# A hybrid encoder in one kernel: the swapped B table's copies moved behind x's evictions, and another order of y, layer norm, gelu and the first output projection

## The chip, the cores and the metric

The kernel runs on one core of a Trainium2 chip, as one program. The metric is the device time of one execution in microseconds (us); less is better. The kernel before takes 1248.14 us (median of 3 runs, 1248.09 to 1248.31). A difference of 0.2%, about 2.5 us, is what a measurement of this kernel can tell from no change.

Names: PE is TensorE, DVE is VectorE, ACT is ScalarE, POOL is GpSimd, and SP is the engine whose queue starts most transfers. Each engine works through its own instructions in the order of the program; a wait of one instruction holds all that stand behind it on the same engine.

## What is computed

Two layers over 512 tokens of 1024 channels, each followed by a gated feed-forward block of width 2816. Only the first layer's mixer matters here. Cut to that:

```python
def conv_ssm_layer(h, w_in, ...):
    z = h @ w_in                                   # 512 x 1536
    za, zg, u = z[..., :512], z[..., 512:1024], z[..., 1024:]
    ya = conformer_conv(za, zg, ...)               # silu(layer_norm(conv31(za * sigmoid(zg)) + conv_b))
    yb = s5_mixer(u, ...)                          # two scans (forward, backward), gelu, gated linear unit
    return jnp.concatenate([ya, yb], axis=-1) @ w_out

def s5_mixer(u, ...):
    y = y_fwd + y_bwd + d_skip * u
    y = gelu(y)
    return y * sigmoid(y @ glu_w + glu_b)
...
x = x + conv_ssm_layer(rms_norm(x, g), ...)
x = x + swiglu_ffn(rms_norm(x, f), ...)            # then layer 1: neighbourhood attention, and swiglu again
```

Here `h = rms_norm(x, mix_norm[0])`; the kernel scales by the norm after the projection.

## The kernel before

The order on each engine is written out by hand in the code: the framework keeps the order of issue. Matmuls of the later part are done as three products of two halves, high and low (`mm3`, L200 to L203: high by high, low by high, high by low), so each weight chunk is split into `whi` (ACT, L91) and `wlo` (DVE, L93) by `Weights.split`; the twelve chunks of the input projection are used whole, straight from the transfer (`wraw`, three buffers, loaded by SP, L74).

**The start.** `x` comes in as four slices (two tiles named `U` and `an`); the transfers of `x` are issued first, then three weight chunks, then the small tables (`b`, vectors, `c`). `g_params` on DVE works out the state-space coefficients, a chain of about a hundred small operations; its last six (`g_cmul`, L437) make the table `bb`. Two ACT copies then make `bbs`, the table with real and imaginary part exchanged and one sign turned (L568, L569). Behind the call of `g_params` in the program stand 32 transposes of `x` on PE into eight PSUM tiles (L617), and for each of these tiles two ACT evictions: `xg` (scaled by the norm's gain, L620) and `xT` (kept for the residual, L621). The first projection `u` (L668) takes `xg`, four weight chunks and four PSUM tiles that the first four of the eight give up. After the first chunk's turn come four squares on ACT (L662) for the norm's `rsqrt` on DVE, after the second `make_pb(0)` to `make_pb(2)` on DVE (three operations each, L437), which read `bb` and `bbs`, and `piece_t` on PE (L630), which reads `pb`.

**The middle.** Scans, the other two projections (`zg`, `za`, L731) and the tables of the convolution run interleaved, until `an` goes through 64 transposes into `AC` and the convolution runs on PE (L994), four blocks of four groups.

**Behind the convolution.** During the convolution DVE works on `Q`, eight pieces of three operations each (`fused`, L437), the tables of the SSM's output. How many go between two of its other instructions is set by a credit in nanoseconds, `tick(TCONV)` per group, and by `bgV.finish(piece)` where a piece is needed. Each block of the convolution is evicted by DVE with a sum for the layer norm (L1004, L1006). Then:

- `out_y(i, hq)`, four times: 24 matmuls of T and Q against U and the states (L1023, L1026) and one ACT eviction into `yn` (L1029).
- `ln_mean`: four small matmuls `mean` (L1065), two DVE subtractions (L1069), eight ACT squares (L1073). `ln_scale`: one small matmul `var` (L1078), `rsqrt` of twelve DVE operations, then eight scalings, five on DVE (L1084) and three on ACT (L1082).
- `out_t(ct)`: eight transposes `yT` (L1091) and an ACT eviction into `yg`, which has `AC`'s buffer (L1038).
- `out_a(ct)`: eight transposes `cT` (L1091), ACT's Silu (L1101), the high half `mah` (DVE for three of four, L1104, ACT for the last, L1106) and the low half `mal` (DVE, L1107).
- `gelu(c1, c2)`: six steps for two channel tiles in lockstep, alternating between ACT and DVE (L1044 to L1054); it ends with `ygh` (ACT) and `ygl` (DVE), which the trace both calls `ygs`.
- `out_half(p, mah, mal, ...)`: 24 matmuls `wo` of one weight chunk. Then 48 matmuls `glu`, in two chunks of 24, which read `ygs`.

The order of the last ones is written in `MIDS = (2, 0, 3, 1)`: gelu of tiles 0 and 2, half 0, gelu of tiles 1 and 3, half 1; the glu's matmuls take the tiles in the order 0, 2, 1, 3.

```python
    for ct in (0, 2, 1, 3):
        out_t(ct)
    for ct in range(4):
        out_a(ct)
    ...
    for v in MIDS:
        if v < 2:
            out_half(v, mah, mal, True, psa)
        else:
            gelu(*((0, 2), (1, 3))[v - 2])
```

Of the kernel before, what the change touches and what calls it, by code (L numbers as in the profile page):

```python
# [9 lines left out]
F32 = mybir.dt.float32  # L10
F32R = mybir.dt.float32r
I32 = mybir.dt.int32
AF = mybir.ActivationFunctionType
ALU = mybir.AluOpType
# [5 lines left out]

CAP = 3000.0
HV = (4, 4)
TCONV = 1900
TCV = 10
QN, QT = 0, 2
LN, LT, LV = 1, 4, 6
LNA, MAH = (1, 3, 5), (0, 1, 2)
KW, VW = 64, 64
ZT, ZC = 500, -1000
MIDS = (2, 0, 3, 1)  # L30

P = 128
D = 1024
KD = 8
S = 512
# [81 lines left out]
def tile_hybrid_encoder(ctx, tc, x, mix_norm, ffn_norm, ffn_w_gate, ffn_w_up, ffn_w_down,  # L117
# [5 lines left out]
    V, A, PE, PL = nc.vector, nc.scalar, nc.tensor, nc.gpsimd  # L123
# [73 lines left out]
    def tmp(shape, tag, bufs=2, dt=F32):  # L197
        return sm.tile(shape, dt, tag=tag, name=tag, bufs=bufs)
# [120 lines left out]
    bgV = Background(1.0)  # L319
# [10 lines left out]
    mp = mixp.enter_context(tc.tile_pool(name="mp", bufs=1))  # L330
# [174 lines left out]
    def g_params():  # L505
        lr, li = par[:, 0], par[:, 1]
        dt = pg()
        th, si, co = (pg(3 * G).rearrange("p (a g) -> p a g", a=3) for _ in range(3))
        x1 = pg(2 * G).rearrange("p (a g) -> p a g", a=2)
        yield from g_exp(dt, par[:, 2], G)  # L510
        yield tt(x1[:, 0], lr, dt, ALU.mult)
        yield tt(th[:, 0], li, dt, ALU.mult)
        yield ts(x1[:, 1], x1[:, 0], float(LCH), None, ALU.mult, None)
        for i in (1, 2):
            yield ts(th[:, i], th[:, 0], float(LCH ** i), None, ALU.mult, None)
        yield from g_lockstep(g_exp(*(v.rearrange("p a g -> p (a g)") for v in (m8, x1)), 2 * G),
                              g_sincos(*(v.rearrange("p a g -> p (a g)") for v in (si, co, th)), 3 * G))
        V.memset(pw[:, 0, 0], 1.0)
        V.memset(pw[:, 1, 0], 0.0)
        ar, ai = pw[:, 0, 1], pw[:, 1, 1]  # L520
        yield tt(ar, m8[:, 0], co[:, 0], ALU.mult)
        yield tt(ai, m8[:, 0], si[:, 0], ALU.mult)
        V.memset(et[:, 0, 0], 1.0)
        V.memset(et[:, 1, 0], 0.0)
        V.tensor_copy(out=et[:, 0, 1], in_=co[:, 1:3])
        V.tensor_copy(out=et[:, 1, 1], in_=si[:, 1:3])
        t1, t2, den, cr, ci, pr = (pg() for _ in range(6))
        t3, t4 = pg(), pg()
        u1, u2 = (pg(4 * G).rearrange("p (e g) -> p e g", e=4) for _ in range(2))

        def g_coef():
            yield tt(den, lr, lr, ALU.mult)
            yield tt(t1, li, li, ALU.mult)
            yield ts(pr, ar, 1.0, None, ALU.subtract, None)
            yield tt(den, den, t1, ALU.add)
            yield tt(t1, pr, lr, ALU.mult)
            yield tt(t2, ai, li, ALU.mult)
            V.reciprocal(out=den, in_=den)
            yield 280
            yield tt(t3, ai, lr, ALU.mult)  # L540
            yield tt(t4, pr, li, ALU.mult)
            yield tt(t1, t1, t2, ALU.add)
            yield tt(t3, t3, t4, ALU.subtract)
            yield tt(cr, t1, den, ALU.mult)
            yield tt(ci, t3, den, ALU.mult)

        def g_pow():
            for base, n in ((1, 1), (2, 2), (4, 4)):
                sh = [P, n, G]
                br, bi = (pw[:, q, base].unsqueeze(1).to_broadcast(sh) for q in range(2))  # L550
                yield from g_cmul(pw[:, 0, base + 1:base + 1 + n], pw[:, 1, base + 1:base + 1 + n],
                                  pw[:, 0, 1:1 + n], pw[:, 1, 1:1 + n], br, bi, u1[:, 0:n], u2[:, 0:n])

        yield from g_lockstep(g_coef(), g_pow())
        f, b = slice(0, 64), slice(64, 128)
        for q in range(2):
            V.tensor_copy(out=pwP[f, q].rearrange("p g (t j) -> p j t g", t=2),
                          in_=pw[f, q, 7::-1].rearrange("p (j t) g -> p j t g", t=2))
            yield cost(256)
            V.tensor_copy(out=pwP[b, q].rearrange("p g (t j) -> p j t g", t=2),  # L560
                          in_=pw[b, q, 0:8].rearrange("p (j t) g -> p j t g", t=2))
            yield cost(256)
        yield from g_phase()
        sh = [P, G, 16]
        w1, w2 = pbt(sh), pbt(sh)
        yield from g_cmul(bb[:, :, 0], bb[:, :, 1], cr.unsqueeze(2).to_broadcast(sh),
                          ci.unsqueeze(2).to_broadcast(sh), braw[0], braw[1], w1, w2)
        A.activation(out=bbs[:, :, 0], in_=bb[:, :, 1], func=AF.Copy, scale=-1.0)  # L568
        A.activation(out=bbs[:, :, 1], in_=bb[:, :, 0], func=AF.Copy)  # L569

    def g_phase():

# [83 lines left out]
    for i in range(4):  # L656
        w = W.next()
        W.ahead()
        if i == 0:
            ss = tmp([P, 4], "hrs", 1)  # L660
            for j in range(4):
                A.activation(out=un.rearrange("p g j c -> p (g j c)")[:, 0:D], in_=xn[j], func=AF.Square,  # L662
                             accum_out=ss[:, j:j + 1])
        for kk in range(2):
            k = 2 * i + kk
            for j in range(4):
                c = slice(j * P, (j + 1) * P)
                PE.matmul(out=pu[j], lhsT=xg[:, k, c], rhs=w[:, kk], start=(k == 0), stop=(k == 7))  # L668
# [25 lines left out]
        if i == 2:  # L694
            for r in range(2):
                ps = psb("ct")
                for t in range(4):
# [3 lines left out]
                             scale=-1.0 if r else 1.0)  # L701
# [103 lines left out]
    S2 = pt([P, 2, G, NCH], "S2")  # L805
# [206 lines left out]
    def out_y(i, hq, between=None):  # L1012
        for key in ((i, hq), (i + 2, hq)):
            if key in job_q:
                bgV.finish(job_q[key])
        ps = psb("y")
        for gi in range(4):
            if gi == 2 and between is not None:
                between()
            gs = [h * 16 + i * 8 + hq * 4 + gi for h in range(2)]  # L1020
            o = [ps[64 * h:64 * h + 64, gi * P:(gi + 1) * P] for h in range(2)]
            for h, g in enumerate(gs):
                PE.matmul(out=o[h], lhsT=U[:, g], rhs=T[:, :, g], start=True, stop=False)  # L1023
            for r in range(2):
                for h, g in enumerate(gs):
                    PE.matmul(out=o[h], lhsT=S2[:, r, g],  # L1026
                              rhs=Q[g // 8][:, hq, r, gi].rearrange("p t c -> p (t c)"),
                              start=False, stop=(r == 1))
        A.activation(out=yn[:, :, i * 8 + hq * 4:i * 8 + hq * 4 + 4],  # L1029
                     in_=ps.rearrange("p (g t c) -> p t g c", g=4, t=LCH), func=AF.Copy)  # L1030
# [4 lines left out]
    def out_t(ct):  # L1035
        ps = psb("yT")
        chan(yn, ct, ps)
        A.activation(out=yg[:, ct], in_=ps, func=AF.Copy)  # L1038
# [17 lines left out]
    def gelu(*cts):  # L1056
        for _ in g_lockstep(*(g_gelu(ct) for ct in cts)):
            pass
# [35 lines left out]
    def mix_tile(n):  # L1094
        return lp.tile([P, 4, S], F32R, tag="Q", name=n, bufs=4)

    def out_a(ct):
        ps = psa("cT")
        chan(yc, ct, ps)
        y = tmp([P, S], ("sq", "sqacc")[ct % 2])  # L1100
        A.activation(out=y, in_=ps, func=AF.Silu, scale=col[:, R_LG + ct:R_LG + ct + 1],  # L1101
                     bias=col[:, R_LB + ct:R_LB + ct + 1])
        if ct in MAH:
            V.tensor_copy(out=mah[:, ct], in_=y)  # L1104
        else:
            A.activation(out=mah[:, ct], in_=y, func=AF.Copy)  # L1106
        V.tensor_tensor(out=mal[:, ct], in0=y, in1=mah[:, ct].bitcast(F32), op=ALU.subtract)  # L1107

    out_y(0, 0)
    bgV.finish(job_q[1, 0])  # L1110
    ln_mean()
    out_y(0, 1)
    out_y(1, 0)
    out_y(1, 1)
    ln_scale()
    ygs = mp.tile([P, 2, 4, S], F32R, tag="S2", name="ygs")
    ygh, ygl = ygs[:, 0], ygs[:, 1]
    mah, mal = mix_tile("mah"), mix_tile("mal")
    for ct in (0, 2, 1, 3):
        out_t(ct)  # L1120
    for ct in range(4):
        out_a(ct)

    po = {}

    def out_half(p, mh, ml, first, ps_of=None):
        wh, wl = W.next()
        W.ahead()
        for mi in range(2):
            m = 2 * p + mi  # L1130
            if first:
                po[m] = ps_of("wo")
            c = slice(mi * P, mi * P + P)
            for k in range(4):
                mm3(po[m], wh[:, k, c], wl[:, k, c], mh[:, k], ml[:, k], first and k == 0,
                    not first and k == 3)

    for v in MIDS:
        if v < 2:
            out_half(v, mah, mal, True, psa)  # L1140
        else:
            gelu(*((0, 2), (1, 3))[v - 2])
    mbh, mbl = mix_tile("mbh"), mix_tile("mbl")
    for p2 in range(2):
        wh, wl = W.next()
# [403 lines left out]
```

## Time and profile before

| | |
|---|---|
| median of 3 runs | 1248.14 us (1248.09 to 1248.31) |
| the profiled execution, its own time | 1248.74 us |
| its span, first to last instruction | 1247.0 us |
| PE busy | 1198.9 us, 96% of the span |
| DVE busy | 664.7 us, 53% |
| ACT busy | 474.9 us, 38% |
| POOL busy | 40.2 us, 3% |
| DMA, mean rate | 95 GB/s |

How to read it: of the span, 48 us are left in which PE has no matmul, and the page's forty slices of 31 us show where: PE's digit is 2 in the first slice and 7 in the sixth and seventh, about 156 to 218 us; elsewhere it is 9, but for an 8 in the last. Both places that the change touches lie in these slices. A busy PE is not one at its peak: the granted clock stands beside it, in tenths 7 in the first slice, 8 in the sixth and 7 in the seventh, 9 elsewhere.

### The profile page before, as it was taken

To read this page: it belongs to the slowest core of one execution; us is meant where nothing else is said; L and a number is where in the kernel's file an instruction comes from. 1 tells how busy PE (TensorE), PEld (TensorE's weight loads), DVE (VectorE), ACT (ScalarE), POOL (GpSimd) and SP (SyncE) were. 2 spreads that over 40 slices of the span, in tenths; PEclk is the share of its full clock that TensorE was granted. 3 is DMA by queue.
4 is the path that set the end of the run, shared out by engine and by line. 5 is a ranking of instruction groups with operands and counts; after the bars stand their busy time and mean duration, and the time that the engine had idled before them with its cause. 6 is when DMAs were issued, how large, how long until landed. Compare 5 with 4: busy or idle time off the path is not lost.

```text
span 1247.0 us, 16100 instructions
## 1 busy us (share of the span) xinstructions
PE 1198.9 (96%) x6427; PEld 952.8 (76%) x6427; DVE 664.7 (53%) x1113; ACT 474.9 (38%) x837; POOL 40.2 (3%) x90
## 2 busy tenths in 40 slices
PE   2999977999999999999999999999999999999998
PEld 2465566888888888888888887678888888888886
DVE  8489986675444444433336753766544444442322
ACT  0667484543323223222225455744322332221120
POOL 1100100000000000000000001520000000000000
PEclk7999987999999999999999999999999999999999
DMA  7411231333333333233344453313333333323321
GB/s 156 75 41 56 76 73 35 101 89 98 91 96 102 101 102 95 82 93 93 93 142 158 119 169 91 102 39 101 85 102 102 95 91 99 89 100 101 119 101 34
DMA packets 173154, 118.04 MB, mean 95 GB/s; under 512 B 21193, under 2 KB 153593, under 8 KB 173080
## 3 DMA queue, kind: packets, MB, share of 16 engines
q1 hardware_dynamic: 172616, 115.92, 32.1%
q10 hardware_dynamic: 400, 1.07, 0.4%
q8 instruction: 50, 0.82, 0.3%
q14 instruction: 24, 0.20, 0.1%
q0 software_dynamic: 64, 0.03, 0.0%
HBM read 109.04 MB, written 7.96 MB: 94 GB/s over the span
## 4 chain that ended last, share of the span: by engine, by line
PE 87%; DVE 10%; ACT 2%; issue 1%; DMA 0%; DVEq 0%; POOL 0%; POOLq 0%
PE up L201 6%; PE gate L203 6%; PE up L203 6%; PE gate L201 6%; PE gate L202 6%; PE up L202 6%; PE qkv L1414 4%; PE qkv L1416 4%; PE qkv L1415 4%; PE dn L203 3%; PE dn L201 3%; PE dn L202 3%; PE dn L1515 3%; PE dn L1513 3%; PE dn L1514 3%; DVE work L437 3%
## 5 line engine op out<-in xcount | busy, mean ns | idle before, releaser
L93 DVE TENSOR_TENSOR wlo<-wraw,whi 128x1024 fp32r<-128x1024 f32 x176 | 213.0, 1213 | 256.2 <-ACT whi L91 254.7
L91 ACT ACTIVATE whi<-wraw 128x1024 fp32r<-128x1024 f32 x176 | 183.5, 1044 | 282.3 <-issue 113.6
L201 PE MATMUL gate<-xgh,whi 128*128 128x512 f32 x352 | 137.2, 390 | 0.0
L201 PE MATMUL up<-xgh,whi 128*128 128x512 f32 x352 | 137.1, 390 | 0.0
L203 PE MATMUL gate<-xgh,wlo 128*128 128x512 f32 x352 | 137.0, 389 | 0.0
L203 PE MATMUL up<-xgh,wlo 128*128 128x512 f32 x352 | 137.0, 389 | 0.0
L202 PE MATMUL gate<-xgl,whi 128*128 128x512 f32 x352 | 136.9, 389 | 0.0
L202 PE MATMUL up<-xgl,whi 128*128 128x512 f32 x352 | 136.9, 389 | 0.0
L1198 DVE TENSOR_TENSOR fu<-up,rstdB 128x512 f32<-128x512 f32 x44 | 30.4, 691 | 113.4 <-PE up L203 113.4
L1200 ACT ACTIVATE gh<-fu 128x512 fp32r<-128x512 f32 x44 | 27.8, 632 | 151.2 <-DVE fu L1199 151.2
L203 PEld LDWEIGHTS up<-xgh,wlo 128*128 128x128 f32 x352 | 66.1, 188 | 13.7
L201 PEld LDWEIGHTS gate<-xgh,whi 128*128 128x128 f32 x352 | 66.1, 188 | 13.7
L202 PEld LDWEIGHTS up<-xgl,whi 128*128 128x128 f32 x352 | 66.1, 188 | 13.8
L202 PEld LDWEIGHTS gate<-xgl,whi 128*128 128x128 f32 x352 | 66.1, 188 | 13.7
L203 PEld LDWEIGHTS gate<-xgh,wlo 128*128 128x128 f32 x352 | 66.0, 188 | 13.8
L201 PEld LDWEIGHTS up<-xgh,whi 128*128 128x128 f32 x352 | 66.0, 188 | 13.6
L201 PE MATMUL dn<-gh,whi 128*128 128x512 f32 x176 | 69.3, 394 | 0.0
L202 PE MATMUL dn<-gl,whi 128*128 128x512 f32 x176 | 69.3, 394 | 0.0
L203 PE MATMUL dn<-gh,wlo 128*128 128x512 f32 x176 | 69.3, 394 | 0.0
L1515 PE MATMUL dn<-whi,gl 128*128 128x512 f32 x176 | 69.2, 393 | 0.0
L1513 PE MATMUL dn<-whi,gh 128*128 128x512 f32 x176 | 69.0, 392 | 0.0
L1414 PE MATMUL qkv<-whi,xgh 128*128 128x512 f32 x176 | 68.8, 391 | 0.0
(299 smaller groups left out, 2017.9 us busy)
## 6 DMA issues: line engine op xcount, KB each, us to landing
wraw<-in_ffn_w_gate_dram SPq DMA_DIRECT2D x44, 512.0 KB
wraw<-in_ffn_w_up_dram SPq DMA_DIRECT2D x44, 512.0 KB
wraw<-in_ffn_w_down_dram SPq DMA_DIRECT2D x38, 512.0 KB
wraw<-in_na_w_qkv_dram SPq DMA_DIRECT2D x24, 512.0 KB
wraw<-in_ab_w_in_dram SPq DMA_DIRECT2D x12, 512.0 KB
bt<-bd SPq DMA_DIRECT2D x8, 640.0 KB
wraw<-in_ab_w_out_dram SPq DMA_DIRECT2D x8, 512.0 KB
wraw<-in_na_w_out_dram SPq DMA_DIRECT2D x8, 512.0 KB
```

Source lines behind the costliest of these rows:

```text
L91: self.nc.scalar.activation(out=hi, in_=raw, func=AF.Copy)
L93: eng.tensor_tensor(out=lo, in0=raw, in1=hi.bitcast(F32), op=ALU.subtract)
L201: PE.matmul(out=o, lhsT=lh, rhs=rh, start=start, stop=False)
L202: PE.matmul(out=o, lhsT=lh, rhs=rl, start=False, stop=False)
L203: PE.matmul(out=o, lhsT=ll, rhs=rh, start=False, stop=stop)
L437: V.tensor_tensor(out=o, in0=a, in1=b, op=op)
L1414: PE.matmul(out=pq[j], lhsT=lh, rhs=wh[:, kk], start=(k == 0), stop=False)
L1415: PE.matmul(out=pq[j], lhsT=lh, rhs=wl[:, kk], start=False, stop=False)
L1416: PE.matmul(out=pq[j], lhsT=ll, rhs=wh[:, kk], start=False, stop=(k == 7))
L1513: PE.matmul(out=pd[j], lhsT=gh[:, k, c], rhs=wh[:, kk], start=(k == 0), stop=False)
L1514: PE.matmul(out=pd[j], lhsT=gh[:, k, c], rhs=wl[:, kk], start=False, stop=False)
L1515: PE.matmul(out=pd[j], lhsT=gl[:, k, c], rhs=wh[:, kk], start=False, stop=(k == NF - 1))
```

## The change

1. The two copies of `bbs` are taken out of `g_params` and issued on ACT behind the evictions of `x` and the four squares.
2. `TCONV` goes from 1900 to 2200, so more pieces of `Q` stand between the convolution's groups.
3. Behind the convolution `out_y(1, 1)`, the `yT` transposes and both gelus are issued behind half 0; `ln_scale` and `out_a` move ahead of them. All four `mah` are made on ACT, and the four `mal` are issued on DVE together, behind the four.

```diff
-TCONV = 1900
+TCONV = 2200
...
-LNA, MAH = (1, 3, 5), (0, 1, 2)
+LNA = (1, 3, 5)
...
-MIDS = (2, 0, 3, 1)
...
         yield from g_cmul(bb[:, :, 0], bb[:, :, 1], cr.unsqueeze(2).to_broadcast(sh),
                           ci.unsqueeze(2).to_broadcast(sh), braw[0], braw[1], w1, w2)
-        A.activation(out=bbs[:, :, 0], in_=bb[:, :, 1], func=AF.Copy, scale=-1.0)
-        A.activation(out=bbs[:, :, 1], in_=bb[:, :, 0], func=AF.Copy)
...
             for j in range(4):
                 A.activation(out=un.rearrange("p g j c -> p (g j c)")[:, 0:D], in_=xn[j], func=AF.Square,
                              accum_out=ss[:, j:j + 1])
+            A.activation(out=bbs[:, :, 0], in_=bb[:, :, 1], func=AF.Copy, scale=-1.0)
+            A.activation(out=bbs[:, :, 1], in_=bb[:, :, 0], func=AF.Copy)
...
+    ya = {}
+
     def out_a(ct):
         ps = psa("cT")
         chan(yc, ct, ps)
-        y = tmp([P, S], ("sq", "sqacc")[ct % 2])
+        y = ya[ct] = tmp([P, S], ("sq", "sqacc")[ct % 2])
         A.activation(out=y, in_=ps, func=AF.Silu, scale=col[:, R_LG + ct:R_LG + ct + 1],
                      bias=col[:, R_LB + ct:R_LB + ct + 1])
-        if ct in MAH:
-            V.tensor_copy(out=mah[:, ct], in_=y)
-        else:
-            A.activation(out=mah[:, ct], in_=y, func=AF.Copy)
-        V.tensor_tensor(out=mal[:, ct], in0=y, in1=mah[:, ct].bitcast(F32), op=ALU.subtract)
+        A.activation(out=mah[:, ct], in_=y, func=AF.Copy)
+
+    def out_a_low(ct):
+        V.tensor_tensor(out=mal[:, ct], in0=ya.pop(ct), in1=mah[:, ct].bitcast(F32), op=ALU.subtract)
...
     out_y(1, 0)
-    out_y(1, 1)
     ln_scale()
-    ygs = mp.tile([P, 2, 4, S], F32R, tag="S2", name="ygs")
-    ygh, ygl = ygs[:, 0], ygs[:, 1]
     mah, mal = mix_tile("mah"), mix_tile("mal")
-    for ct in (0, 2, 1, 3):
-        out_t(ct)
     for ct in range(4):
         out_a(ct)
+    bgV.finish(job_q[1, 1])
+    for ct in range(4):
+        out_a_low(ct)
...
-    for v in MIDS:
-        if v < 2:
-            out_half(v, mah, mal, True, psa)
-        else:
-            gelu(*((0, 2), (1, 3))[v - 2])
+    out_half(0, mah, mal, True, psa)
+    out_y(1, 1)
+    ygs = mp.tile([P, 2, 4, S], F32R, tag="S2", name="ygs")
+    ygh, ygl = ygs[:, 0], ygs[:, 1]
+    for ct in (0, 2, 1, 3):
+        out_t(ct)
+    gelu(0, 2)
+    gelu(1, 3)
+    out_half(1, mah, mal, True, psa)
```

What this does to the order is shown at three places. The first is ACT at the start, before; the sixteen evictions alternate as their first two rows do.

```order
L608 ACTIVATE col<-vec_171 128x16
L568 ACTIVATE bbs<-bb 128x8x64
L569 ACTIVATE bbs<-bb 128x8x64
L620 ACTIVATE xg<-xT,col 128x512
L621 ACTIVATE xT<-xT 128x512
...
L662 ACTIVATE un_ppb,hrs<-U 128x1024 x2
L662 ACTIVATE un_ppb,hrs<-an 128x1024 x2
L682 ACTIVATE col<-vec 128x34
```

The same place with the change:

```order
L605 ACTIVATE col<-vec_171 128x16
L617 ACTIVATE xg<-xT,col 128x512
L618 ACTIVATE xT<-xT 128x512
...
L659 ACTIVATE un_ppb,hrs<-U 128x1024 x2
L659 ACTIVATE un_ppb,hrs<-an 128x1024 x2
L661 ACTIVATE bbs<-bb 128x8x64
L662 ACTIVATE bbs<-bb 128x8x64
L681 ACTIVATE col<-vec 128x34
```

The two copies have moved behind the evictions and the squares; nothing else moved on ACT there, and nothing on the other engines.

The second place is ACT behind the convolution, from the layer norm's scaling to the first gelu, before (`sq` and `sqacc` are the Silu's results, `AC` the evicted `yT`, `whi` the split of the next weight chunk).

```order
L1029 ACTIVATE yn<-y 128x8x64 x3
L1082 ACTIVATE an<-an,rs_y 128x256 x3
L1038 ACTIVATE AC<-yT 128x512 x4
L1101 ACTIVATE sq<-cT,col 128x512
L1101 ACTIVATE sqacc<-cT,col 128x512
...
L1106 ACTIVATE mah<-sqacc 128x512
L1044 ACTIVATE sq<-AC 128x512 x2
```

The same place with the change:

```order
L1028 ACTIVATE yn<-y 128x8x64 x2
L1081 ACTIVATE an<-an,rs_y 128x256 x3
L1102 ACTIVATE sq<-cT,col 128x512
L1104 ACTIVATE mah<-sq 128x512
L1102 ACTIVATE sqacc<-cT,col 128x512
L1104 ACTIVATE mah<-sqacc 128x512
...
L90 ACTIVATE whi<-wraw 128x1024
L1028 ACTIVATE yn<-y 128x8x64
L1037 ACTIVATE AC<-yT 128x512 x4
L1043 ACTIVATE sq<-AC 128x512 x2
```

The last `yn`, the four `AC` evictions and the gelu stand behind the four Silus now, each Silu has its `mah` behind it, and a weight split stands ahead of the last `yn`. On PE the order is correspondingly `var`, `cT`, 24 `wo`, the last 24 `y`, `yT`, 24 `wo`, `glu`, where it was the last `y`, `var`, `yT`, `cT`, 48 `wo`, `glu`.

The third place is DVE at the end of the convolution, from the weight splits on, before:

```order
L93 TENSOR_TENSOR wlo<-wraw,whi 128x1024 x2
L1004 TENSOR_TENSOR an<-conv,rstdB 128x8x64
L1006 TENSOR_REDUCE lns<-an 128x8
L437 TENSOR_TENSOR wq<-pwQ,CTs 128x1024
L437 TENSOR_TENSOR Q<-Q,wq 128x1024
L437 TENSOR_TENSOR Q<-pwQ,CT 128x1024
L1004 TENSOR_TENSOR an<-conv,rstdB 128x8x64
L1006 TENSOR_REDUCE lns<-an 128x8
L1069 TENSOR_TENSOR an<-an,mean 128x1024 x2
L437 TENSOR_TENSOR wq<-pwQ,CTs 128x1024
L437 TENSOR_TENSOR Q<-Q,wq 128x1024
```

The same place with the change:

```order
L92 TENSOR_TENSOR wlo<-wraw,whi 128x1024 x2
L1003 TENSOR_TENSOR an<-conv,rstdB 128x8x64
L1005 TENSOR_REDUCE lns<-an 128x8
L436 TENSOR_TENSOR wq<-pwQ,CTs 128x1024
L436 TENSOR_TENSOR Q<-Q,wq 128x1024
L1003 TENSOR_TENSOR an<-conv,rstdB 128x8x64
L1005 TENSOR_REDUCE lns<-an 128x8
L1068 TENSOR_TENSOR an<-an,mean 128x1024 x2
```

All 24 operations of `Q` now stand ahead of the mean's subtraction; two stood behind it. Of these, one operation now stands ahead of the first evicted block, a place where DVE waited, and one more of the 24 between the table of groups 10 and 11 (`tcb`) and the last evicted block.

## Rows read from the trace of the kernel before

**Rows 1.** The page's chain that ended last, by engine, whole span.
```profile
PE 87%; DVE 10%; ACT 2%; issue 1%; DMA 0%; DVEq 0%; POOL 0%; POOLq 0%
```

**Rows 2.** Windows: engine busy in each stretch, clock, DMA share, GB/s.
```profile
core 0: us, PE busy (x) PEld busy (x) DVE busy (x) ACT busy (x) POOL busy (x), PEclk, DMA share, GB/s
9.00:13.00 4.00, 3.89 (x19) 3.92 (x20) 3.93 (x27) 0.00 (x0) 0.00 (x0) 1.00 1.02 229
...
18.00:19.00 1.00, 0.00 (x0) 0.00 (x0) 0.93 (x5) 0.00 (x0) 0.00 (x0) 0.78 0.12 8
...
32.00:35.50 3.50, 3.50 (x4) 1.44 (x5) 0.00 (x0) 3.50 (x7) 0.00 (x0) 0.50 0.00 0
...
80.00:120.00 40.00, 40.00 (x351) 22.94 (x350) 38.96 (x45) 25.45 (x58) 0.00 (x0) 1.00 0.18 53
```

**Rows 3.** Timeline of ACT at the start: start us, duration us, instruction, [idle before].
```profile
29.72 0.63 ACT L568 ACTIVATE bbs<-bb 128x512 f32<-128x512 f32 x1 [22.57 <-DVE bb L437]
...
30.78 0.67 ACT L620 ACTIVATE xg<-xT,col 128x512 f32<-128x512 f32 x1
...
31.82 0.69 ACT L620 ACTIVATE xg<-xT,col 128x512 f32<-128x512 f32 x1
```

**Rows 4.** Timeline of PE at the start.
```profile
12.55 3.18 PE L617 MATMUL xT<-ident,an 128*128 128x128 f32 x16
31.99 15.79 PE L668 MATMUL u<-wraw,xg 128*128 128x512 f32 x32 [16.26 <-ACT xT L621]
...
56.10 1.04 PE L630 MATMUL P<-ident,pb 128*128 128x128 f32 x8
```

**Rows 5.** Timeline of DVE at the start.
```profile
43.99 0.17 DVE L220 TENSOR_SCALAR rs_a<-hrs 128x4 f32<-128x4 f32 x1 [14.30 <-ACT un_ppb L662]
...
46.45 1.22 DVE L437 TENSOR_TENSOR pb<-pwP,bb 128x1024 f32<-128x1024 f32 x1
```

**Rows 6.** Timeline of SP's queue at the start.
```profile
5.33 4.56 SPq L74 DMA_DIRECT2D wraw<-in_ab_w_in_dram  x3
```

**Rows 7.** Two tiles' instructions: duration ns min/median/max, first and last start us.
```profile
L617 PE MATMUL xT<-ident,U x16: 421/421/448, 9.1 to 12.3; 128*128 128x128 f32 x16
...
L630 PE MATMUL P<-ident,pb x24: 272/273/273, 56.1 to 76.0; 128*128 128x128 f32 x24
```

**Rows 8.** Timeline of PE behind the convolution.
```profile
193.20 0.59 PE L1065 MATMUL mean<-lns,wpad 128*128 128x8 f32 x2 [4.46 <-DVE lns L1006]
...
204.51 0.39 PE L1078 MATMUL var<-lnq,wpad 128*128 128x8 f32 x2
...
208.89 2.77 PE L1091 MATMUL cT<-ident,an 64*128 64x64 f32 x32 [2.43 <-DVE an L1084]
211.78 0.79 PE L201 MATMUL wo<-mah,whi 128*128 128x512 f32 x1
...
219.74 0.39 PE L201 MATMUL wo<-mah,whi 128*128 128x512 f32 x1
...
225.18 0.39 PE L201 MATMUL glu<-ygs,whi 128*128 128x512 f32 x1
```

**Rows 9.** Windows behind the convolution; columns as in rows 2.
```profile
190.00:199.00 9.00, 5.80 (x52) 5.78 (x54) 7.82 (x8) 3.30 (x16) 0.00 (x0) 0.50 0.09 31
...
209.00:216.50 7.50, 7.38 (x42) 5.86 (x43) 5.00 (x10) 6.74 (x13) 0.00 (x0) 0.55 0.00 0
```

**Rows 10.** Timeline of DVE behind the convolution.
```profile
196.10 1.22 DVE L437 TENSOR_TENSOR wq<-pwQ,CTs 128x1024 f32<-128x1024 f32 x1
...
223.35 1.29 DVE L1054 TENSOR_TENSOR ygs<-AC,ygs 128x512 fp32r<-128x512 f32 x2
```

**Rows 11.** Timeline of ACT behind the convolution.
```profile
208.57 2.03 ACT L1038 ACTIVATE AC<-yT 128x512 f32<-128x512 f32 x4
210.48 0.79 ACT L1101 ACTIVATE sq<-cT,col 128x512 f32<-128x512 f32 x1
...
213.90 1.35 ACT L1044 ACTIVATE sq<-AC 128x512 f32<-128x512 f32 x2
...
219.31 1.13 ACT L1044 ACTIVATE sq<-AC 128x512 f32<-128x512 f32 x2
```

## The prediction

> **What bounds the kernel now.** I read the page's chain first: PE carries 87% of it, DVE 10% [rows 1]. The page's slices show PE busy from the eighth on, so the later layers stay as they are. What can move lies in the stretches in which PE waits, and I read those in the timelines of the engines, with the windows beside them for the clock.
>
> Two places matter. At the start ACT sits idle for 22.57 us until DVE has made `bb`, because the two `bbs` copies stand at the head of its queue [rows 3]. The evictions of x stand behind them, although the transposes that fill their PSUM tiles ended at 15.73 us (12.55 + 3.18), and PE waits 16.26 us for the first pair [rows 4]. Behind the convolution PE waits for the layer norm: 4.46 us before the last `mean` matmuls and 2.43 us before `cT` [rows 8], and after such waits it works at half clock, 0.50 granted from 190 to 199 us and 0.55 from 209 to 216.5 us [rows 9], which is 1.2 GHz for nearly all of both.
>
> **Part 1, the copies of bbs.** They take 1.1 us of ACT and stay; what changes is who waits for them.
> - The first of the eight PSUM tiles is complete with the first of the last eight transposes, which are half of the row at 12.55: 12.55 + 1.59 + 0.4 = 14.5 us. ACT's first eviction can start there and not at 30.78 [rows 3].
> - PE's first `u` matmul came 1.2 us behind the first eviction (31.99 against 30.78), since it also needs that pair's PSUM tile. So it starts at 15.7 us, 16.3 us earlier.
> - The clock. Before, the first 3.5 us of `u` ran at 0.50 [rows 2]: 1.75 us lost. With the change `u` follows the transposes without a gap, and I expect full clock. But the first four matmuls are then paced by ACT's pairs, 1.04 us apart (30.78 to 31.82), where one takes 0.88 us at full clock (16 matmuls, 32 records, in 15.79 us less the 1.75 lost): 0.5 us is lost again. Net gain 1.2 us.
> - Sum: -17.5 us to the end of the second weight chunk.
>
> The window from 9 to 13 us grants a clock of 1.00 [rows 2], yet the transposes there take 421 ns each where those of the same shape at 56 us take 273 ns [rows 7]. So the record is no proof that PE is at full clock at 15.7 us. [...] If `u` starts at half clock as before, the 1.2 us are not won.
>
> What could stop the gain behind this point:
> - `bbs` itself. The squares end 13.2 us behind the first eviction (30.78 to 43.99), so at 27.7 us; `bb` is there at 29.7 as before (the copy started at 29.72); the copies end at 30.9. On DVE the `rsqrt` no longer waits 14.30 us [rows 5] but starts behind `bb`, takes 2.46 us (43.99 to 46.45), and the second operation of `make_pb(0)`, the first reader of `bbs`, comes at 33.4. Spare: 2.5 us.
> - `pb`. Three operations of 1.22 us bring the first to about 35.8 us; PE wants it 17.5 us earlier than 56.10 [rows 4], at 38.6. Spare: 2.8 us.
> - The first weight chunk. Its landing is not shown. SP issued three chunks from 5.33 us on [rows 6]; the transfers run full at 229 GB/s from 9 to 13 us, and their share falls to 0.12 at 18 to 19 us [rows 2]. So it lands between about 13 and 18.5 us; it is the first of three, and 15.7 is likely in time. At worst it costs 2.8 us.
>
> From 80 to 120 us DVE is busy 38.96 of 40 us and PE fully [rows 2]; both hang on what `u` feeds and nothing on the clock of the wall, so the gain is carried through the middle whole. Bounds for part 1: -17.5 at best, -13.5 (late weights, half clock). I take **-17.3**.
>
> **Part 2, the order behind the convolution.** All times here are in the frame of the trace before; the shift of part 1 comes on top.
> - One more `Q` operation, 1.2 us [rows 10], stands on DVE ahead of the last evicted block, so `mean` comes at 194.4 and not 193.2: +1.2.
> - From `mean` to `var` PE had 11.3 us of `y` (193.20 to 204.51), with three `out_y`. The last one, 2.6 us at full clock, is gone from there: `var` at 203.1, 1.4 us earlier.
> - From `var` to `cT` 4.4 us (rsqrt and scaling; 204.51 to 208.89): `cT` at 207.5.
> - The first `cT` tile takes 0.7 us (2.77 / 4), the Silu 0.8, `mah` on ACT about 0.6 (the four `AC` copies took 2.03 us): first `wo` at 209.7, where before the Silu queued behind the `AC` evictions until 210.48 [rows 11] and `wo` came at 211.78. This is 2.1 us won.
> - Half 0 took 8.0 us (211.78 to 219.74), mostly at half clock. Silu and `mah` follow each other every 1.2 us, no slower than three matmuls at half clock, and PE's wait ahead of `cT` is still there; so 8.0 again: end at 217.7.
> - Now the work that used to be done already: `out_y(1, 1)` 2.6 us and the `yn` eviction 0.75: 221.05. One `yT` tile 0.4, the four `AC` evictions 2.03: gelu starts at 223.5.
> - The gelus. The first pair held ACT for 4.4 us (213.90 to 219.31 less a weight split of 1.0); the second took 5.3 us from its first square to its last `ygl` (219.31 to 223.35 + 1.29), some 0.6 of it behind a split on DVE. So the last `ygl` is there at 223.5 + 4.4 + 4.7 = 232.6.
> - Beside it PE has only the rest of `yT` and half 1, 5.4 us (219.74 to 225.18), until 228.1, and then the glu's first tiles. Before, both halves covered the two gelus. So PE waits about 3 us in all for gelu, and the first 24 `glu` matmuls end 3.2 us behind the last `ygl`: 235.9. Before they ended at 225.18 + 5.44 = 230.6.
> - Sum: **+5.3 us**.
>
> Bounds: where y(0, 1) and half 0 run at full clock, 2.6 and 0.5 us less, +2.2; where `out_y(1, 1)` and the glu's start run at half clock too, 2.6 and 1.5 more, +9.4. The four `mal` issued together cost nothing: half 0 takes each when its `mah` is there, and DVE has nothing else queued. The three casts that DVE loses are in the 1.2 us of ACT.
>
> **Sum.** -17.3 + 5.3 = -12.0 us. The profiled execution took 1248.74 us (span 1247.0 and 1.74 around it), 0.6 more than the median; from it the sum gives 1236.7, and from the median 1248.14 it gives 1236.1.
>
> **The rivals.**
> - *The order behind the convolution costs nothing* (part 2 is 0): the earlier `wo` wins as much as the late gelu loses, because PE, kept busier around `cT`, stays at full clock. For it: both waits ahead of the half-clock stretches are what the order is aimed at. Against it: the wait ahead of `cT` keeps its 4.4 us, and the gelu chain of 9 us has 5.4 us of cover. Time: 1248.1 - 17.3 = 1230.8. Chance 0.13.
> - *Half clock throughout*: PE now waits at `mean`, at `cT`, at `yn` and at the glu, and the trace has half clock after the first two. If it also follows the other two, `y`, half 1 and the glu's start pay, 4 to 5 us more: 1240.9. Chance 0.12.
> - *Late weights, slower than before*: the first weight chunk lands far later than the share of the DMA says, behind the small tables. If it landed at 31.9 us, PE would start where it does now, and only part 2 would be left: 1248.1 + 5.3 = 1253.4. It decides where the chunk lands after 27.7 us. For it: no row shows the landing. Against it: PE's wait is put down to ACT [rows 4], and the queue was nearly empty at 18 to 19 us. Chance 0.03.
> - *The change doesn't do what it says*: the evictions start early but the chain of DVE through `bb`, `pb` and the scans is the true bound, and both parts cancel: within 0.2% of before. Against it: the spare of 2.8 us ahead of `pb`. Chance 0.02.
>
> **How the numbers follow.** The forecast, both parts as summed, has 0.70; its own bounds are 1248.1 - 15.3 = 1232.8 and 1248.1 - 4.1 = 1244.0. The range goes down to the first rival, 1230.8, and up past the second, to 1242.0; what is left out is the two last rivals and the far end of the bounds. A measurement of this kernel can tell about 0.2%, 2.5 us. Faster by more than that: the forecast and the first two rivals, 0.95; within it 0.02; slower 0.03.
>
> **What would show it.** Right: `u` starts near 15.7 us on PE with no wait over 1 us ahead of it; ACT's 22.57 us are gone; the same middle, 17 us earlier; `P` without a wait. Behind the convolution, from the end of the last block on: `var` 1 to 2 us earlier, first `wo` 2 us earlier, and a new wait of PE for `ygs` ahead of or within the first `glu`, of 2 to 4 us. Wrong: PE waiting for the weights or for `pb` at 16 to 40 us (part 1), or no wait at the glu (part 2).

## The result and the profile after

| | median | runs | ratio to before, 95% interval |
|---|---|---|---|
| before | 1248.22 us | 1248.09 to 1248.44 (4) | |
| after | 1236.34 us | 1235.37 to 1237.33 (4) | 0.9905 [0.9887, 0.9922] |

The change takes 11.9 us off by the medians. The profiled execution of after took 1235.37 us with a span of 1233.6, so the two traces to compare differ by 13.4 us in span (1247.0 less 1233.6); that execution is the fastest of its four, and the one of before lies 0.5 us above its median, which makes up the rest.

The page's chain now reads:

```profile
PE 92%; DVE 3%; DMA 2%; SPq 2%; ACT 1%; issue 0%; DVEq 0%; POOL 0%; ACTq 0%; POOLq 0%
```

DVE's share fell from 10% [rows 1] to 3%. At the start the chain now goes back through `u` and SP's transfers of small tables, and no longer through DVE's table chain; but that chain, from 2.8 to 29.7 us, is at most 27 of the some 87 us by which the share fell. Most of the rest lies between 60 and 130 us, where the chain is followed back through PE's projections and not through DVE's tables and scans. The two profiles of trial 2 below, one kernel, show 92% for PE with 5% for DVE, and 86% with 10%, so that part is no effect of the change. The timeline of PE at the start, and of the tile that the transposes fill, the view of [rows 7]:

```profile
11.70 2.90 PE L614 MATMUL xT<-ident,an 128*128 128x128 f32 x16
15.16 14.63 PE L667 MATMUL u<-wraw,xg 128*128 128x512 f32 x32 [0.56 <-ACT xT L618]
...
38.26 1.04 PE L627 MATMUL P<-ident,pb 128*128 128x128 f32 x8
```

```profile
L614 PE MATMUL xT<-ident,an x16: 272/421/421, 11.7 to 14.3; 128*128 128x128 f32 x16
```

ACT and DVE at the start, their timelines:

```profile
13.93 0.69 ACT L617 ACTIVATE xg<-xT,col 128x512 f32<-128x512 f32 x1 [6.76 <-PE xT L614]
...
29.76 0.63 ACT L661 ACTIVATE bbs<-bb 128x512 f32<-128x512 f32 x1 [2.60 <-DVE bb L436]
```

```profile
29.64 0.16 DVE L219 TENSOR_SCALAR rs_a<-hrs 128x4 f32<-128x4 f32 x1
...
33.23 1.22 DVE L436 TENSOR_TENSOR work<-pwP,bbs 128x1024 f32<-128x1024 f32 x1
```

PE waits 0.56 us where it waited 16.26 [rows 4], and ACT's wait for `bb` is 2.60 us where it was 22.57 [rows 3]; it now lies behind the evictions and the squares, and nobody waits for it: the first reader of `bbs` starts at 33.23, 2.3 us behind the copies (29.76 + two of 0.6). `P` comes 17.84 us earlier than before (56.10 to 38.26), without a wait, and this shift holds through the middle: the convolution's last matmuls start 17.84 us earlier too, before and after:

```profile
181.48 2.40 PE L994 MATMUL conv<-tca,AC 128*64 128x128 f32 x40 [1.78 <-ACT tca L762]
163.64 2.40 PE L993 MATMUL conv<-tca,AC 128*64 128x128 f32 x40 [1.78 <-ACT tca L761]
```

Behind the convolution I therefore add 17.84 to after's times when I compare. PE there:

```profile
176.53 0.60 PE L1064 MATMUL mean<-lns,wpad 128*128 128x8 f32 x2 [3.12 <-DVE lns L1005]
...
184.34 0.39 PE L1077 MATMUL var<-lnq,wpad 128*128 128x8 f32 x2
188.80 3.28 PE L1090 MATMUL cT<-ident,an 64*128 64x64 f32 x32 [4.07 <-DVE an L1083]
192.01 0.79 PE L200 MATMUL wo<-mah,whi 128*128 128x512 f32 x1
...
199.62 0.44 PE L1022 MATMUL y<-T,U 128*64 128x128 f32 x4
...
202.40 1.78 PE L1090 MATMUL yT<-ident,yn 64*128 64x64 f32 x32
204.11 0.50 PE L200 MATMUL wo<-mah,whi 128*128 128x512 f32 x1
...
209.68 0.39 PE L200 MATMUL glu<-ygs,whi 128*128 128x512 f32 x1
...
212.54 0.50 PE L200 MATMUL glu<-ygs,whi 128*128 128x512 f32 x1 [1.34 <-ACT ygs L1051]
...
213.27 0.50 PE L201 MATMUL glu<-ygs,whi 128*128 128x512 f32 x1 [0.23 <-DVE ygs L1053]
```

ACT between half 0 and the glu:

```profile
202.51 0.60 ACT L1028 ACTIVATE yn<-y 128x512 f32<-128x512 f32 x1 [6.16 <-PE y L1025]
203.14 2.07 ACT L1037 ACTIVATE AC<-yT 128x512 f32<-128x512 f32 x4
205.06 1.17 ACT L1043 ACTIVATE sq<-AC 128x512 f32<-128x512 f32 x2
```

Compare [rows 11]: the gelu's first square stood at 213.90, with 5.8 us of half 0 and all of half 1 still to come on PE; now it stands at 205.06 (222.90 with the shift), behind half 0, and ACT sits idle for 6.16 us ahead of the last `yn`. So the glu, which came without a wait [rows 8], waits 1.34 and 0.23 us, after six of its matmuls. The windows, columns as in [rows 2]:

```profile
9.00:13.00 4.00, 4.00 (x21) 4.00 (x20) 3.93 (x27) 0.00 (x0) 0.00 (x0) 1.00 1.03 235
...
15.00:20.00 5.00, 4.84 (x10) 1.76 (x11) 4.87 (x29) 5.00 (x11) 0.00 (x0) 1.00 0.81 143
...
176.00:180.00 4.00, 3.47 (x30) 3.45 (x32) 2.83 (x3) 1.58 (x8) 0.00 (x0) 0.50 0.01 4
...
189.00:194.00 5.00, 5.00 (x37) 4.46 (x37) 1.39 (x2) 3.94 (x7) 0.00 (x0) 0.50 0.00 2
195.00:214.00 19.00, 17.21 (x132) 13.48 (x132) 9.60 (x14) 11.93 (x21) 0.00 (x0) 1.00 0.09 28
```

The clock (third figure from the end) is full at `u`, half behind both layer norm waits as before [rows 9], and full from 195 us on, through the wait for the gelu.

### The profile page after: what moved, and what is told of

It is laid out like the page before. It is cut to its first block, busy times and chain, and to the rows that moved or that the text cites. A ratio compares the mean times of both kernels' runs of the same rounds, so it can differ in the third digit from the quotient of the medians.

```text
span 1233.6 us, 16107 instructions
## 1 busy us (share of the span) xinstructions
PE 1198.1 (97%) x6427; PEld 951.3 (77%) x6427; DVE 663.5 (54%) x1110; ACT 476.9 (39%) x840; POOL 41.6 (3%) x90
## 4 chain that ended last, share of the span: by engine, by line
PE 92%; DVE 3%; DMA 2%; SPq 2%; ACT 1%; issue 0%; DVEq 0%; POOL 0%; ACTq 0%; POOLq 0%
PE up L200 6%; PE gate L200 6%; PE gate L202 6%; PE up L202 6%; PE gate L201 6%; PE up L201 6%; PE qkv L1416 4%; PE qkv L1418 4%; PE qkv L1417 4%; PE dn L201 3%; PE dn L202 3%; PE dn L200 3%; PE dn L1517 3%; PE dn L1515 3%; PE dn L1516 3%; PE zg L730 2%
```

## The experiments

Times are medians; the ratio stands against runs of the kernel before on the same chip. Two theories were in the prediction: the copies' place in ACT's queue is worth the whole gain, and the new order costs some 5 us because the gelu comes late. The rivals: the order is free, or the copies' gain needs the order.

**1. The copies alone.** The kernel before with `bbs` moved, and nothing else:

```diff
-        A.activation(out=bbs[:, :, 0], in_=bb[:, :, 1], func=AF.Copy, scale=-1.0)
-        A.activation(out=bbs[:, :, 1], in_=bb[:, :, 0], func=AF.Copy)
...
                              accum_out=ss[:, j:j + 1])
+            A.activation(out=bbs[:, :, 0], in_=bb[:, :, 1], func=AF.Copy, scale=-1.0)
+            A.activation(out=bbs[:, :, 1], in_=bb[:, :, 0], func=AF.Copy)
```

> The kernel before with part 1 alone: the two bbs copies behind x's evictions and the squares, the old order behind the convolution. Theory (two parts that add up: the start wins 17.8 us, the order costs 4.4 us): 1248.2 - 17.8 = 1230.4 us, with u starting at 15.2 us and no wait of PE for ygs. Rival (the two parts hang together, so that a shorter wait behind the convolution carries some of the gain): the copies alone win less, 12 to 14 us, 1234 to 1236.

1230.75 us (1229.94 to 1232.04), 0.9857 [0.9843, 0.9870]. The interval lies below the change's own: half of the change does more than all of it.

**2. The order alone**, the change with the copies left at the head of ACT's queue (trial 1's diff, the other way round, on the change).

> The kernel before with part 2 alone: TCONV 2200 and the new order behind the convolution, the copies in their old place. Theory: 1248.2 + 4.4 = 1252.6 us, with PE waiting for ygs inside the first 24 glu matmuls. Rival (the order is free or wins a little, and the whole change is smaller than its first part for another reason, such as the clock at the start): 1247 to 1249.

1256.34 us, 1.0057 [1.0044, 1.0070]: slower, as the theory has it, but 3.7 us over its sum. The profiled execution shows where 2.3 of them lie. SP waits for transfers into the scratch array `kd` before it may load `T` and the convolution's bias; one of these transfers is a small adding DMA of POOL. DMA issues of before and of this kernel, last figure: median us from issue to landing.

```profile
kd<-un_ppb POOLq DMA_DIRECT2D x1, 32.0 KB, 2.4
```

```profile
kd<-un_ppb POOLq DMA_DIRECT2D x1, 32.0 KB, 4.1
```

So the bias comes late, the first block is evicted late (170.85 us against 168.58), and DVE, whose queue has no gap from there to the last block, hands that on to the mean at 196.74, where the sum has 194.4. A last trial took the same kernel again:

> The new order alone, the same kernel as in the second trial, profiled again. There the small adding DMA of POOL into kd took 4.1 us to land, where the kernel before shows 2.4, and the mean came 2.3 us later than the sum had it. Theory: whether it lands after 2.4 or after about 4 us changes from execution to execution. If this profile shows 2.4, the last mean stands at about 194.4 us and not at 196.74, and its time is 1253 to 1254.5 us; with about 4 again, 1255.5 to 1257.5. In either case the mean and the time go together. Rival: the landing has nothing to do with it, and the mean stands at 196 to 197 with a landing of 2.4.

1254.02 us (1253.92 to 1254.87), 1.0045 [1.0031, 1.0059]. The DMA, and PE in this profile and, in the last line, in the first one:

```profile
kd<-un_ppb POOLq DMA_DIRECT2D x1, 32.0 KB, 2.5
```

```profile
194.78 0.59 PE L1064 MATMUL mean<-lns,wpad 128*128 128x8 f32 x2 [3.32 <-DVE lns L1005]
196.74 0.59 PE L1064 MATMUL mean<-lns,wpad 128*128 128x8 f32 x2 [3.12 <-DVE lns L1005]
```

The DMA landed after 2.5 us and the last mean stands at 194.78: DMA, mean and time go together, as expected. The span is 1252.2, 5.2 more than before.

**3. The copies on POOL**, in their old place in the program: only ACT's queue is relieved.

```diff
-        A.activation(out=bbs[:, :, 0], in_=bb[:, :, 1], func=AF.Copy, scale=-1.0)
+        PL.tensor_scalar(out=bbs[:, :, 0], in0=bb[:, :, 1], scalar1=-1.0, scalar2=1.0, op0=ALU.mult, op1=ALU.mult)
```

The second copy is changed in the same way.

> The kernel before, with the two bbs copies left in their place in the program but done by POOL, so that ACT's queue holds no wait for bb. Theory (it is the place of the waiting copies in ACT's queue that held the evictions, and nothing else of the move): ACT evicts at 14 us and the gain is that of the copies' move, 17.8 us, less up to 1 us if POOL, which took 2.0 us for an operation of this size, brings bbs too late for make_pb: 1230.4 to 1231.4. Rival (the gain comes from the squares or from DVE being served earlier by the moved copies): under 5 us, 1243 or more.

1229.39 us (1229.26 to 1229.57), 0.9845 [0.9830, 0.9860]. The copies need not come late, only out of the way of the evictions. That it lies 1.4 us under trial 1 is no effect shown: the two intervals overlap, and the landing that trial 2 tells of took 3.8 us in trial 1's profile and 2.4 in this one.

**4. The layer norm ahead of y(1,1).** On top of trial 1, `ln_scale()` and `out_y(1, 1)` change places, so that y(1,1) may fill PE's wait ahead of `cT`.

```diff
-    out_y(1, 1)
     ln_scale()
+    out_y(1, 1)
```

> Part 1, and in the old order one swap alone: ln_scale ahead of out_y(1, 1), so that y(1, 1) lies in PE's wait between var and cT. Theory (behind the convolution the wait ahead of cT, and the half clock behind it, is what can be won; gelu must keep both halves as its cover): var 2.6 us earlier, the first wo 1.5 us earlier and part of cT and half 0 at full clock: 1.5 to 5 us under the copies alone, 1225.5 to 1229, most likely 1227.5. Rival (ACT, with yn, AC and the Silus in one queue, sets the first wo): as the copies alone, 1230.4.

1234.73 us, 0.9888 [0.9874, 0.9901]: a miss, 4 us slower than trial 1. PE and DVE:

```profile
184.82 0.38 PE L1026 MATMUL y<-Q,S 128*64 128x128 f32 x2
190.99 0.90 PE L1026 MATMUL y<-Q,S 128*64 128x128 f32 x5 [5.79 <-DVE Q L437]
```

```profile
187.14 1.40 DVE L1084 TENSOR_SCALAR an<-an,rs_y 128x256 f32<-128x256 f32 x5
188.46 1.22 DVE L437 TENSOR_TENSOR wq<-pwQ,CTs 128x1024 f32<-128x1024 f32 x1
```

`out_y(1, 1)` itself asks for the last piece of `Q`; issued behind `ln_scale`, the piece fell behind the `rsqrt` and the scalings on DVE, and y(1,1) waited 5.79 us for it. This is what the raised `TCONV` and the `bgV.finish` of the change guard against.

**5. Half 0 as cover.** On the change:

```diff
-    out_half(0, mah, mal, True, psa)
     out_y(1, 1)
...
     gelu(0, 2)
+    out_half(0, mah, mal, True, psa)
     gelu(1, 3)
```

> The changed kernel with the first half of the out-projection moved behind y(1,1) and the yT tiles, so that both halves lie beside the gelus. Theory: the cost of the new order is the cover that half 0 used to give the gelu. cT at 188.8 us as in the changed kernel, y(1,1) from 192.0 to 194.7 (up to 196 at half clock), yT, half 0 and half 1 (10.8 us) to about 207, the last ygl at about 207 as well, so the second 24 glu matmuls start at 212 to 213.5 and not at 217.2: 1231 to 1233 us. Rival: the gelu chain ends as late as before because ACT is the bound (Silu, mah, yn, AC in one queue), and half 0 only takes another place: 1235 us or more.

1233.93 us (1232.63 to 1235.79), 0.9883 [0.9869, 0.9896]; the profiled execution, its fastest, is 2.7 us shorter in span than after's. PE:

```profile
192.21 0.69 PE L1022 MATMUL y<-T,U 128*64 128x128 f32 x4
...
209.08 0.39 PE L200 MATMUL glu<-ygs,whi 128*128 128x512 f32 x1
```

The glu's wait is gone (PE runs from half 1 into it at 209.08, and the last `ygl` ends at 209.25). But y(1,1), now right behind `cT`, has a granted clock of 0.50 until 195 us and takes 4.1 us (192.21 to 196.3) where it takes 2.6 at full clock, and the median falls 1 us short of the expectation: half 0 was cover, worth 2.4 us by the medians, and not all of the cost.

**6. The place of y(1,1).** The change with `out_y(1, 1)` alone moved back to right behind `ln_scale()`. Its `Q` is ready there, since the change paces it.

```diff
     ln_scale()
+    out_y(1, 1)
     mah, mal = mix_tile("mah"), mix_tile("mal")
...
     out_half(0, mah, mal, True, psa)
-    out_y(1, 1)
```

> The changed kernel with y(1,1) alone moved back, from behind half 0 to directly behind the layer norm's var; yT, gelu and the halves stay as the change has them. Theory: y(1,1) then lies in PE's wait of 4.07 us ahead of cT and costs nothing there; half 0 keeps its end at about 199.5 us (its pace is ACT's Silu and mah, 1.33 us for each), yT starts at 199.4 and not at 202.4, gelu's first square at 202.1 and not at 205.06, and the second 24 glu matmuls at 214.2 and not at 217.2: 3.0 us less, 1232.5 to 1234.3 us. If half 0 is paced by the clock instead and the clock now stays up, it ends 2 us earlier and the time is 1231 to 1232.5. Rival: y(1,1)'s place is free, the late gelu is due to ACT alone: 1235.5 or more.

1234.18 us (1232.16 to 1235.01), 0.9883 [0.9870, 0.9896], within the expectation. PE:

```profile
184.62 0.44 PE L1022 MATMUL y<-T,U 128*64 128x128 f32 x4
...
199.17 1.63 PE L1090 MATMUL yT<-ident,yn 64*128 64x64 f32 x32
...
209.32 0.49 PE L200 MATMUL glu<-ygs,whi 128*128 128x512 f32 x1 [1.50 <-ACT ygs L1051]
```

y(1,1) vanishes in the wait ahead of `cT`, the glu's wait comes 3.2 us earlier, and half 0, though it began 1 us earlier (191.03 against 192.01), ends only 0.45 earlier. So do the four `mah` on ACT, each 1.33 us behind the one before (the last ends at 194.97, in after at 195.40): they pace it.

**7. The pace of Q alone**: `TCONV = 2200` in place of 1900, on top of trial 1.

> The moved copies alone with the pace of Q beside the convolution raised from 1900 to 2200, and the old order behind it. Theory: one more Q operation ahead of the last evicted block makes the mean 1.2 us later, the rest stays: 1231.5 to 1232.5 us, the last mean matmuls 1.2 us later than where the pace is 1900 and the DMA of the convolution's bias lands at the same time. Rival: the pace costs nothing, because the operation goes into DVE's wait ahead of the first evicted block: 1230 to 1231.

1231.34 us (1230.10 to 1232.53), 0.9861 [0.9847, 0.9874]. This settles nothing: it lies between the two expectations. The last mean at 176.23 is 0.9 us later than trial 3's at 175.37, where the DMA landed as early.

**8. Trial 4 with the last Q finished first.**

```diff
+    for key in ((1, 1), (3, 1)):
+        bgV.finish(job_q[key])
     ln_scale()
     out_y(1, 1)
```

> The last trial (rsqrt and scaling issued ahead of y(1,1), with the moved copies) with the last two Q pieces finished ahead of the rsqrt. Theory: the miss of that trial was Q alone. y(1,1) follows var at once, fills PE while DVE makes the scaled an, cT comes at about 189 us and not at 191.6 (moved copies alone), and PE keeps full clock in half 0: 1226 to 1228.5 us, ahead of all kernels so far. Rival: the yn and AC evictions of y(1,1) now stand in ACT's queue when the Silu wants it, and eat the gain: 1229.5 to 1231.

1227.46 us (1226.69 to 1228.54), 0.9830 [0.9816, 0.9843]: as expected, and 8.9 us ahead of the change. PE, and a window:

```profile
184.30 0.39 PE L1078 MATMUL var<-lnq,wpad 128*128 128x8 f32 x2
...
192.06 0.49 PE L201 MATMUL wo<-mah,whi 128*128 128x512 f32 x1 [0.46 <-DVE mah L1104]
...
204.35 0.39 PE L201 MATMUL glu<-ygs,whi 128*128 128x512 f32 x1
```

```profile
186.00:194.00 8.00, 6.64 (x97) 5.40 (x94) 4.69 (x16) 6.78 (x13) 0.00 (x0) 1.00 0.01 2
```

All five of its times lie below all four of trial 1. The glu starts at 204.35 without a wait, 5.3 us earlier than in the change, and the clock stays full through `cT` and half 0.

**9. Work in PE's wait.** On top of trial 1, matmuls that nobody needs stand between the `mean` matmuls, n1 and n2 of them. They write a PSUM tile of their own.

```diff
+            for _ in range((0, n1, n2, 0)[b]):
+                PE.matmul(out=fl[:, 0:P], lhsT=pair, rhs=pair, start=True, stop=True)
```

With 10 and 38:

> The moved copies alone, with 48 matmuls of 128 columns added (10 behind the second mean matmul, 38 behind the third; they write a PSUM tile that nobody reads) so that PE works through its wait ahead of the last mean. Theory: the wait is what halves the clock of the y matmuls behind it; two groups of y that took 1.28 us take 0.66, in other executions up to four: 1228 to 1229.5 us, no granted clock of 0.50 between 174 and 182 us. Rival: the granted clock falls there whatever PE does, or the added matmuls run past the wait: 1230.5 to 1232.

1232.97 us, 0.9872 [0.9859, 0.9886], a miss in the time: 2.2 us slower than trial 1, since the added work ran past the wait, as the rival has it in its second half. PE:

```profile
171.53 8.73 PE L1068 MATMUL fl<-wpad 128*128 128x128 f32 x76
180.10 0.29 PE L1066 MATMUL mean<-lns,wpad 128*128 128x8 f32 x2
...
188.33 0.39 PE L1081 MATMUL var<-lnq,wpad 128*128 128x8 f32 x2
```

Each took 0.23 us, the last block's sums were there at 175.31, and so the mean came 4.8 us late (the expectation of the next trial puts this at 3.2). But the clock held at 1.00, and mean to var took 8.23 us, where it took 11.31 before (193.20 to 204.51, [rows 8]) and 9.91 in trial 1. With 4 and 17:

> The moved copies alone with the same 21 added matmuls, which now end ahead of the last block's sums. Theory: last time 38 of them ran 3.2 us past the wait and cost more than the clock gave; the clock itself stayed at 1.00, mean to var took 8.2 us and not 9.9. With 17 the last mean comes when it does without them: 1230.75 - 1.7 = 1229.0, between 1228 and 1229.8. Rival: the time does not depend on the clock of y, because the layer norm is bound by DVE and ACT: 1230.5 to 1231.5.

1228.87 us (1227.44 to 1230.08), 0.9842 [0.9829, 0.9856], within the expectation, though its interval overlaps trial 1's. Mean to var is 8.23 us again (177.93 to 186.16). In this execution POOL's DMA landed after 3.8 us, PE had a wait of 2.00 us ahead of the added work, and they ran partly at half clock; the `y` behind them ran at full clock.

**10. Both together**, trial 8 with 4 and 17 added matmuls.

> The trial with the early Q (rsqrt ahead of y(1,1), moved copies) and 21 added matmuls (4 and 17) in the two waits ahead of the last mean, sized by the last trial of them: 0.23 us each, 17 take 3.9 us of the 4.46 us wait. Theory: the clock stays at 1.00 through y(0,1), which took two groups of 1.28 us instead of 0.66 in the early-Q trial's trace; mean to var 5.7 us and not 7.3: 1225 to 1226.5 us. Rival: the rest of the wait (0.5 us) or the added work itself costs what the clock gives back: 1227 or more.

1225.83 us (1224.78 to 1228.47), 0.9822 [0.9808, 0.9835]. Mean to var took 5.71 us (175.55 to 181.26) and trial 8's 7.32. Four of its five runs lie below all five of trial 8, but the intervals overlap. It beats the change by 10.5 us and before by 22.5.

## Why the prediction was right

It said 1236.1 us and the median is 1236.34; the sign, the two parts and the mechanism of each held. That the two agree to 0.3 us is in part luck. By the spans it said -12.0 and the traces show -13.4: both parts came out better by half a microsecond to one, and after's median lies 1 us above its profiled execution.

**Part 1, predicted -17.3 with -17.5 as its best, measured -17.84.** `u` started at 15.16 where the sum had 15.7, with a wait of 0.56 us. The step that was off is the first, and by chance of the execution: the sum takes over the landing of x from the one trace of before. PE's first transposes of x, before and after:

```profile
9.11 3.65 PE L617 MATMUL xT<-ident,U 128*128 128x128 f32 x16 [3.46 <-DMA U<-in_x_dram]
8.26 3.65 PE L614 MATMUL xT<-ident,U 128*128 128x128 f32 x16 [2.57 <-DMA U<-in_x_dram]
```

Those of `an` follow 0.85 us earlier as well (12.55 [rows 4] to 11.70), and ACT's first eviction came 2.23 us behind their start where the sum had 2.0: at 13.93 and not 14.5. In all fourteen profiles the first transpose starts between 7.55 and 9.11 us, latest in the one that the sum was read from; in the eleven with the copies out of the way ACT's first eviction lies between 13.76 and 14.33. The rest of the steps stand as put: `u` at full clock (14.63 us against 14.04 + 0.5), the copies behind the squares at 29.76 (29.7), the second `make_pb` operation at 33.23 (33.4), `P` at 38.26 without a wait (38.6), no wait for the weights. Trial 1's 17.6 us (1248.3 less 1230.75) and trial 3's 18.9 show the part by itself.

The caution about the clock's record was needed: from 9 to 13 us it grants 1.00 in after as well, while the transposes still take 421 ns. The Trainium skill ("TensorE: Matmul & The Clock Gate", Part 1, the caveats on the trace's clock events) says that on trn2 these events have been seen to be unreliable, and the trace agrees with it here.

**Part 2, predicted +5.3, measured +4.45 in after and +5.2 in the order alone.** Step by step, in the frame of before (after shifted by 17.84; the order alone is trial 2's second profile, unshifted: its `u` starts at 32.01, that of before at 31.99):

| | predicted | after | order alone |
|---|---|---|---|
| last `mean` | 194.4 | 194.37 | 194.78 |
| `var` | 203.1 | 202.18 | 202.91 |
| `cT` | 207.5 | 206.64 | 207.37 |
| first `wo` | 209.7 | 209.85 | 210.58 |
| half 0 ends | 217.7 | 217.46 | 218.16 |
| gelu's first square | 223.5 | 222.90 | 223.60 |
| last `ygl` ends | 232.6 | 231.66 | 232.36 |
| second 24 `glu` start (before: 230.62) | 235.9 | 235.07 | 235.82 |

Every step is within 1 us. The largest differences are `var`, which is 0.9 us early in after because fewer groups of `y` ran at half clock, and the first `wo`, 3.2 us behind `cT` where I had 2.2. There the sum had the wrong path: it let `wo` follow the Silu and the `mah` of the first tile, which was ready at 191.41 in after, but PE takes all four `cT` tiles first, and at half clock these last until 192.0. `yT` did not wait for the `yn` of y(1,1), which saved 0.4. Half 0 took 7.6 us against 8.0, and trial 6 shows that ACT sets this, as the step on Silu and `mah` allowed.

Two of the signs that it named came out of their bounds: `var` came 2.3 us earlier in after (1.6 in the order alone) where it had 1 to 2, and PE's new wait in the glu is 1.57 us where it had 2 to 4. Of the 4.45 us, 2.34 are lost when the glu starts (209.68 with the shift, against 225.18) and 2.11 within its first 24 matmuls, which took 7.55 us against 5.44.

**The rivals.** That the order costs nothing is refuted twice: the interval of the order alone is above 1 in both its measurements, and the copies alone beat the whole change by 5.6 us in the median. Half clock throughout fell with the window from 195 to 214 us, 1.00. Late weights and cancelling fell with the start.

**What stands behind the cost of part 2.** Trials 5 and 6 each give back 2.2 to 2.4 us in the medians, about half of it, by the two routes that the sum named: gelu loses half 0 as cover, and y(1,1) with its `yT` stands between half 0 and gelu instead of in the wait ahead of `cT`. Their intervals still overlap the change's own, so their size rests on the traces, where the second 24 `glu` start at 214.52 and 214.07 us and not at 217.23; whether the two add up was not run. Both keep the raised `TCONV`, which makes the mean 1.2 us late (194.37 against 193.20). The wait ahead of `cT` stayed, and grew, 4.07 us against 2.43 [rows 8]. Trial 8 keeps the idea of an early `var` and fills the wait with y(1,1): there the same idea gains 3.3 us over trial 1.

## What to carry to other kernels

When an engine with a queue in order shows a long wait, ask what stands behind the waiting instruction: here two copies of 0.6 us held sixteen evictions and through them the whole kernel by 17.6 us (trial 1), and moving them, or giving them to an idle engine, won this alone. When work is brought forward behind a wait, list what it displaces and where the displaced work now lies: an order that starts `wo` 1 to 2 us earlier lost 4.5 to 5.2 us, most of it because it pushed the one thing the next stage waits for, the gelu, behind it. Bundle changes only after each has been timed by itself.

## What the runs showed of the hardware that was not expected

- POOL's small adding DMA of 32 KB landed after 2.3 to 2.5 us in ten of the profiles and after 3.8 to 4.1 in four (trials 1, 2, 8 and the second of 9), for the same code too (trial 2 shows both). In trial 2's two profiles the last mean moved by 1.96 us with it, and the span by 2.4. The Trainium skill ("SBUF — State Buffer", on the DMA setup-cost knee) gives every transfer a roughly fixed 2 us; the lower value is near it, the higher one is not told there.
- The half clock behind the same wait lasts for a different part of the same twelve groups of `y`: mean to var took 11.31 us before, 10.44 in trial 3 and 9.91 in trial 1, and 8.23 with PE kept busy. So the price of that wait's clock was 1.7 to 3.1 us, by chance of the execution. With the DMA this makes differences of 1 to 3 us between profiles that no edit caused.
- In trial 10 the clock fell to 0.50 at 190 to 192 us, behind two waits of 0.45 and 0.22 us; in trial 8, with waits of 0.46 and 0.23 at the same places, it stayed at 1.00. Why is open.
